# A two-block trunk on one core: lower weights subtracted on VectorE in the feed-forwards, and a bias table stored once and read shifted

## The chip, the cores and the metric

One Trainium2 core runs the whole program in one launch. The metric is the device time of that launch in microseconds: the median of three runs of the kernel before is 3242.26 (3242.16 to 3242.72). TensorE does the matrix products, VectorE (DVE) and ScalarE (ACT) the element-wise work, GpSimd (POOL) some of it, and SyncE (SP) issues most DMAs.

## The reference, cut to what matters

Two models run one after the other on 512 tokens of width 1024 in float32, each of two layers: a hybrid of two attentions with a convolutional feed-forward, then a state-space model beside windowed attention with another feed-forward.

```
def conv_ffn(h, w_up, conv_w, conv_b, w_down):          # first model
    u = h @ w_up                                         # 1024 -> 2 * 2816
    c = conv_b + sum over k < 3 of conv_w[k] * up[:, k:k + s]
    a, val = split(c, 2)
    return (gelu(a) * val) @ w_down                      # 2816 -> 1024

x = x + rms_norm(mixed @ w_out, attn_post_gain)          # a norm behind each half of a layer
h = rms_norm(x, ffn_pre_gain)
x = x + rms_norm(conv_ffn(h, ...), ffn_post_gain)

rel = arange(KEY_SPAN)[None, :] - WINDOW - arange(ATTN_BLOCK)[:, None]        # second model
band_bias = rel_bias[t5_bucket(rel)].transpose(2, 0, 1)   # (16 heads, 128 queries, 384 keys)
```

The bias depends on key minus query alone, so a head has one row of values, and the table's row for a query is that row shifted by the query's place.

## The kernel before, in words

**Exact products out of two halves.** Every weight block (128 x 128) and every activation is held as a rounded part and what is left of it: `wh` and `wl`, `h` and `hl` (`ah`, `al` for the products of a feed-forward). A product takes three matmuls (`mm3`, lines 489 to 491): `wh` with `h`, `wl` with `h`, `wh` with `hl`, all 512 columns wide.

**The stream of weights.** The host packs the weight blocks in the order of use into 460 chunks of eight blocks (512 KB), so TensorE spends 24 matmuls on a chunk. `Stream` brings them in. When the first block of chunk c is asked for, `load` issues the raw loads up to chunk c + 6 on SP (four buffers `wraw`), and `conv` turns chunk c + 3 into its halves (four buffers each of `wh` and `wl`): ScalarE writes the negated raw weights into `wl` (line 311), GpSimd issues a DMA that adds the weights from memory to it, and ScalarE rounds the raw weights into `wh` (line 316; GpSimd does that in the attention stages). Each engine works through its instructions in the order in which this code issues them (the schedule is manual), and so does each DMA queue: an instruction that waits holds up all behind it.

**The stages around the change.** A layer of the first model ends with the product with `w_out` (eight outputs), `post_norm`, a feed-forward, and `post_norm` again. `post_norm` sums squares (`sq`, `stat`), takes the root on ScalarE, spreads the factor over the partitions by four transposes (`statb`), and then for each of eight tiles scales `y`, adds it to `x` (VectorE for even tiles, GpSimd for odd ones), and splits `x` into `h` (ScalarE) and `hl` (VectorE). `keep_warm` gives TensorE small matmuls (`warm`) meanwhile. Behind it, `dense_group` works on four accumulators at once, block row by block row, over four chunks, so that it can begin with the first `h`; the squares for the next norm (`sq`) are taken between its block rows.

A feed-forward is 22 pairs of outputs (`pair`, two chunks each) with a product down (`down`, eleven chunks) behind pair 12 and one behind the last. An output of the first model is scaled (`u`, line 1225, VectorE), multiplied and biased (`c`, ScalarE), and gets two convolution steps (lines 1230 and 1232, VectorE); a pair then gets its gelu (ScalarE), product, rounded half `ah` (ScalarE) and lower half `al` (VectorE), deferred to the following blocks of weights. The second model's pair has one convolved output (lines 1851 to 1860) and one that is only scaled (`up`).

**The bias table.** `bias_table` is a generator that others step with `side.step`. It makes the 16 rows by one matmul (`btab`), stores them, loads each head back shifted by one element per partition (`brev`), turns the order of the partitions round by a matmul with an exchange matrix (`bex`), copies that on ScalarE (`bout`), and stores it to `bias_d`. Its steps stand in the first layer's `w_out` product and, four each, in the four calls of `post_norm`. The attention of the second model loads `bias_d` head by head.

Of the kernel before, what the change touches and what calls it, by code (L numbers as in the profile page):

```python
# [17 lines left out]
T = 512  # L18
# [6 lines left out]
NB, NO = 2, 2  # L25
XD = 30
GA, GB, GC = 1, 4, 1
NWU, NKW = 13, 6
NEG = -1.0e30
BIG = 3.0e38  # L30
TINY = 1e-30
# [102 lines left out]
assert NTILES % CH == 0  # L134
NCHUNK = NTILES // CH


def _pack_weights(arrs):
    out = np.zeros((NCHUNK, 128, CH, 128), np.float32)
# [13 lines left out]
def _consts():  # L153
    parts = []
    pos = 0

    def add(name, a):
        nonlocal pos
        a = np.asarray(a, np.float32)
        _CS[name] = (pos, a.shape[1])  # L160
        parts.append(a)
        pos += a.shape[1]

    p = np.arange(128)
    r, c = p[:, None], p[None, :]
    add("ident", np.eye(128))
    add("exch", np.eye(128)[::-1])
    add("maskA", np.concatenate([np.where(c > r, 0, NEG), np.where(c <= r, 0, NEG)], 1))
    add("maskC", np.concatenate([np.zeros((128, 384)), np.where(c <= r, 0, NEG)], 1))
    add("le", r <= c)  # L170
    add("ge", r >= c)
    add("gt", r > c)
    add("lt", r < c)
    n = np.arange(32)
    ok = np.stack([((n * 16 + 31)[None, :] <= (128 * i + p)[:, None]) & (n < 31)[None, :] for i in range(4)], 1)
    add("c01", ok.reshape(128, 128))
    add("cneg", np.where(ok, 0, NEG).reshape(128, 128))
    add("invf", (10000.0 ** (-(p % 32) / 32.0))[:, None])
    add("sign", np.where(p % 64 < 32, -1.0, 1.0)[:, None])
    return np.concatenate(parts, 1)  # L180
# [66 lines left out]
def trunk_kernel(ctx: ExitStack, tc: tile.TileContext, xT, positions, wts, cst_d, oh_d, rb_d, cw1_d,  # L247
# [14 lines left out]
    def big(name, dt=F32):  # L262
        return pools["t"].tile([128, T], dt, tag="t", name=name)
# [7 lines left out]
    def bank(name, hold=False):  # L271
        b = banks.pop(0)
        t = psum.tile([128, T], F32, tag=f"b{b}", name=name)
        if hold:
            held[id(t)] = (b, t)
        else:
            banks.append(b)
        return t
# [7 lines left out]
    class Stream:  # L286
        LOAD, CONV = 7, 3

        def __init__(self):
            self.t = 0  # L290
            self.loaded = 0
            self.conved = 0
            self.raw = {}
            self.hl = {}
            self.later = []

        def load(self, upto):
            while self.loaded < min(upto, NCHUNK):
# [3 lines left out]
                self.raw[c] = r  # L302
                self.loaded += 1

        def conv(self, upto):
            while self.conved < min(upto, NCHUNK):
                c = self.conved
                r = self.raw.pop(c)
                h = wpool.tile([128, CH * 128], F32R, tag="wh", name="wh", bufs=4)
                lo = wpool.tile([128, CH * 128], F32R, tag="wl", name="wl", bufs=4)  # L310
                A.activation(lo, r, AF.Copy, scale=-1.0)  # L311
                G.dma_start(out=lo, in_=wts[c], accum_op=OP.add)  # L312
                if busy["act"]:
                    G.tensor_copy(h, r)
                else:
                    A.activation(h, r, AF.Copy)  # L316
                self.hl[c] = (h, lo)
                self.conved += 1

        def defer(self, n, fn):  # L320

# [13 lines left out]
        def next(self, key):  # L335
            self.due(self.t)
            c, i = divmod(self.t, CH)
            if i == 0:
                self.load(c + self.LOAD)
                self.conv(c + self.CONV + 1)  # L340
                self.hl.pop(c - 1, None)
            name, l, r, cols = PLAN[self.t]
            assert (name, l, r) == key[:3], (PLAN[self.t], key)
            self.t += 1
            h, lo = self.hl[c]
            s = slice(128 * i, 128 * i + 128)
            return h[:, s], lo[:, s]
# [39 lines left out]
    def C(name):  # L387
        o, n = _CS[name]
        return cst[:, o:o + n]
# [394 lines left out]
    def layer1(l, x, hs, sq, gnext, side):  # L784
# [417 lines left out]

        x = load_x()
        for m in range(KT):
            if l == 0 and m in (1, 3, 4):
                side.step(1)
            g = dense(key("w_out", l), ms, out_evac)
            if m == KT - 1:
                run_some(g, 4)
                sq2.sums(1)  # L1210
                warm_sqrt()
            run(g)
# [23 lines left out]
            return f  # L1236

        def pair(i):
            if i == 0:
                dense_group(key("ffn_w_up", l), hs, [conv(0, "a0"), conv(FT, "v0"), conv(1, "a1"),  # L1240
                                                     conv(FT + 1, "v1")],
                            sq3, st3, x)
                x.clear()
            elif i > 1:
                run(dense(key("ffn_w_up", l), hs, conv(i, f"a{i}")))
                run(dense(key("ffn_w_up", l), hs, conv(FT + i, f"v{i}")))
            later(i, gated)
# [81 lines left out]

    def post_norm(x, ys, gcol, sq, gnext, side):  # L1330

        side.step(1)
        r4 = rstd_a(sq, D, act=True)
        side.step(1)
        R = spread(r4)
        side.step(2)
        keep_warm(NKW)
        hs, sqn, f = prep(x, gnext)
        for m in range(KT):
            y = ys[m]  # L1340
            V.scalar_tensor_tensor(y, y, gcol[:, m:m + 1], R, op0=OP.mult, op1=OP.mult)
            (V if m % 2 == 0 else G).tensor_add(x[m], x[m], y)
            if m:
                f(m - 1)
        f(KT - 1)
        free(R)
        return hs, sqn


    bias_d = dpool.tile([128, 16, 384], F32, name="bias_d")  # L1350

    def bias_table():

        oh = big("oh")
        nc.sync.dma_start(oh[0:33, :], oh_d)
        rb = small(16, "rb", bufs=2)
        nc.sync.dma_start(rb[0:32, :], rb_d)
        V.memset(rb[32:33, :], NEG)
        yield
        ps = bank("btab")  # L1360
        PE.matmul(ps[0:16, :], rb[0:33, :], oh[0:33, :], start=True, stop=True)
        tb_ = big("btab")
        V.tensor_copy(tb_[0:16, :], ps[0:16, :])
        tab_d = dpool.tile([16, T], F32, name="tab_d")
        nc.sync.dma_start(tab_d, tb_[0:16, :])
        rev = {}
        for h in range(18):
            if h < 16:
                rev[h] = big("brev")
                nc.sync.dma_start(rev[h][:, 0:384], bass.AP(  # L1370
                    tensor=tab_d.tensor, offset=tab_d.offset + h * T, ap=[[1, 128], [1, 384]]))
            if h >= 2:
                pb = bank("bex")
                PE.matmul(pb[:, 0:384], C("exch"), rev.pop(h - 2)[:, 0:384], start=True, stop=True)
                o = big("bout")
                A.activation(o[:, 0:384], pb[:, 0:384], AF.Copy)
                nc.sync.dma_start(bias_d[:, h - 2, :], o[:, 0:384])
            yield

    masks = []  # L1380
# [7 lines left out]
    def layer2(l, x, hs, sq, gnext):  # L1388
# [398 lines left out]
        def load_bias(h):  # L1787
            if h < 16:
                bias[h] = big("bias")
                nc.sync.dma_start(bias[h][:, 0:384], bias_d[:, h, :])  # L1790

        bias["load"] = load_bias
        load_bias(0)
# [218 lines left out]
```

## Time and profile before

| | |
|---|---|
| median of three runs | 3242.26 us |
| the profiled execution | 3243.99 us, its span 3242.2 us |
| mean granted TensorE clock | 0.980 |
| chunks of weights | 460, each loaded raw (512 KB) and added once more (512 KB) |
| DMA traffic | 547.30 MB, of it 241.20 MB in the queue of the adding DMAs |

A busy TensorE is not TensorE at its peak; a DMA share is the mean of 16 engines, rough where it goes over 1. Idle time of an engine that nobody waits for costs nothing. A wait for several semaphores is put down to the one that came last.

### The profile page before, as it was taken

To read this page: it belongs to the slowest core of one execution; us is meant where nothing else is said; L and a number is where in the kernel's file an instruction comes from. 1 tells how busy PE (TensorE), PEld (TensorE's weight loads), DVE (VectorE), ACT (ScalarE), POOL (GpSimd) and SP (SyncE) were. 2 spreads that over 40 slices of the span, in tenths; PEclk is the share of its full clock that TensorE was granted. 3 is DMA by queue.
4 is the path that set the end of the run, shared out by engine and by line. 5 is a ranking of instruction groups with operands and counts; after the bars stand their busy time and mean duration, and the time that the engine had idled before them with its cause. 6 is when DMAs were issued, how large, how long until landed. Compare 5 with 4: busy or idle time off the path is not lost. (4 is left out here: it accounts for less than half of the span.)

```text
span 3242.2 us, 40684 instructions
## 1 busy us (share of the span) xinstructions
PE 3104.8 (96%) x14604; PEld 2542.0 (78%) x14604; DVE 1681.9 (52%) x3431; ACT 1885.8 (58%) x3288; POOL 758.1 (23%) x770
## 2 busy tenths in 40 slices
PE   8999999999999999999999889999999988999998
PEld 7878878887778877888786668788888666878887
DVE  5577355153577735424376786331326678734132
ACT  4568556464457756645467577554556766755453
POOL 2222211111222211111125432111112552211110
PEclk9999999999999999999999999999999999999999
DMA  9744769887864487989775435789897534478975
GB/s 272 173 105 92 189 175 207 194 192 198 228 161 110 86 216 182 203 190 221 181 177 117 107 87 115 197 193 220 194 227 167 127 89 105 108 195 206 221 185 139
DMA packets 170277, 547.30 MB, mean 169 GB/s; under 512 B 20011, under 2 KB 29227, under 8 KB 170076
## 3 DMA queue, kind: packets, MB, share of 16 engines
q0 software_dynamic: 66240, 241.20, 43.9%
q1 hardware_dynamic: 103836, 303.50, 27.0%
q8 instruction: 116, 1.90, 0.2%
q14 instruction: 85, 0.70, 0.1%
HBM read 516.81 MB, written 19.96 MB: 166 GB/s over the span
## 5 line engine op out<-in xcount | busy, mean ns | idle before, releaser
L490 PE MATMUL acc<-h,wl 128*128 128x512 f32 x2464 | 975.2, 396 | 34.1 <-DMA wl<-in_wts 34.0
L489 PE MATMUL acc<-h,wh 128*128 128x512 f32 x2464 | 997.8, 405 | 3.5 <-DVE dm L1670 2.1
L491 PE MATMUL acc<-hl,wh 128*128 128x512 f32 x2464 | 973.3, 395 | 0.1
L312 POOL DMA_DIRECT2D wl<-in_wts x460 | 398.6, 867 | 2037.6 <-ACT wl L311 1845.3
L311 ACT ACTIVATE wl<-wraw 128x1024 fp32r<-128x1024 f32 x460 | 482.8, 1050 | 283.3 <-PE acc L490 257.6
L490 PEld LDWEIGHTS acc<-h,wl 128*128 128x128 f32 x2464 | 471.1, 191 | 133.4 <-DMA wl<-in_wts 40.8
L491 PEld LDWEIGHTS acc<-hl,wh 128*128 128x128 f32 x2464 | 469.8, 191 | 101.7 <-DVE hl L404 1.0
L489 PEld LDWEIGHTS acc<-h,wh 128*128 128x128 f32 x2464 | 471.5, 191 | 99.5 <-issue 5.3
L316 ACT ACTIVATE wh<-wraw 128x1024 fp32r<-128x1024 f32 x400 | 417.4, 1043 | 0.0
L489 PE MATMUL acc<-ah,wh 128*128 128x512 f32 x704 | 274.2, 390 | 0.0
L491 PE MATMUL acc<-al,wh 128*128 128x512 f32 x704 | 273.9, 389 | 0.0
L490 PE MATMUL acc<-ah,wl 128*128 128x512 f32 x704 | 273.9, 389 | 0.0
L674 PE MATMUL pt<-cst,p 128*128 128x128 f32 x752 | 143.6, 278 | 25.6 <-ACT p L1939 10.8
L1229 ACT ACTIVATE c<-u,prm 128x512 f32<-128x512 f32 x88 | 71.2, 815 | 144.3 <-DVE u L1225 144.3
L491 PEld LDWEIGHTS acc<-al,wh 128*128 128x128 f32 x704 | 132.1, 188 | 27.5
L489 PEld LDWEIGHTS acc<-ah,wh 128*128 128x128 f32 x704 | 132.1, 188 | 27.4
L490 PEld LDWEIGHTS acc<-ah,wl 128*128 128x128 f32 x704 | 132.1, 188 | 27.4
L1225 DVE TENSOR_TENSOR u<-acc,R 128x512 f32<-128x512 f32 x88 | 59.9, 687 | 172.5 <-PE acc L491 172.5
L1085 ACT ACTIVATE p<-p,nm 128x128 f32<-128x128 f32 x192 | 102.1, 532 | 62.6 <-DVE nm L1083 60.7
L680 ACT ACTIVATE pth<-pt 128x256 fp32r<-128x256 f32 (+2 forms) x320 | 130.8, 411 | 9.3 <-PE pt L674 6.8
L674 PEld LDWEIGHTS pt<-cst,p 128*128 128x128 f32 x752 | 93.0, 141 | 52.8 <-ACT p L1939 19.0
L1417 DVE SCALAR_TENSOR_TENSOR c<-u,prm,c 128x510 f32<-128x510 f32 (+2 forms) x120 | 98.5, 821 | 41.0 <-POOL c L1411 37.6
(334 smaller groups left out, 4944.9 us busy)
## 6 DMA issues: line engine op xcount, KB each, us to landing
wraw<-in_wts SPq DMA_DIRECT2D x460, 512.0 KB, 6.7
wl<-in_wts POOLq DMA_DIRECT2D x460, 512.0 KB, 7.2
bias<-bias_d SPq DMA_DIRECT2D x32, 192.0 KB, 2.5
x<-in_xT SPq DMA_DIRECT2D x16, 256.0 KB, 8.2
cw<-in_cw SPq DMA_DIRECT2D x16, 256.0 KB, 4.7
xf<-x SPq DMA_DIRECT2D x16, 256.0 KB, 2.2
x<-xf SPq DMA_DIRECT2D x16, 256.0 KB, 10.6
xs<-x SPq DMA_DIRECT2D x16, 256.0 KB, 5.7
```

The lines of the kernel that those rows point to most:

```text
L311: A.activation(lo, r, AF.Copy, scale=-1.0)
L312: G.dma_start(out=lo, in_=wts[c], accum_op=OP.add)
L316: A.activation(h, r, AF.Copy)
L489: PE.matmul(acc, wh, xh, start=first, stop=False)
L490: PE.matmul(acc, wl, xh, start=False, stop=False)
L491: PE.matmul(acc, wh, xl, start=False, stop=last)
L674: PE.transpose(pt[:, 128 * n:128 * n + 128], t[:, 128 * (kb - b0):128 * (kb - b0) + 128], ident)
L680: A.activation(th[:, 0:w], pt[:, 0:w], AF.Copy)
L1085: A.activation(p[:, 0:w], p[:, 0:w], AF.Exp, bias=nm[:, col:col + 1], scale=-1.0, accum_out=den[:, col:col + 1])
L1225: V.tensor_mul(u, acc, st3["R"])
L1229: A.activation(c, u, AF.Identity, bias=cb[:, idx:idx + 1], scale=cw[:, 88 + idx:89 + idx])
L1417: V.scalar_tensor_tensor(c[:, lo:hi], u[:, lo + d:hi + d], cw[:, 12 * k + idx:12 * k + idx + 1], c[:, lo:hi], op0=OP.mult, op1=OP.add)
```

## The change

In `conv`, chunks that `BYV` marks get their `wl` as raw minus `wh` by a VectorE instruction in place of the negation and the adding DMA, and their `wh` always from ScalarE. Marked are the first eight chunks and every chunk that belongs to a feed-forward together with the three before it: 260 of 460. A subtraction is issued one chunk later than the rounding that it needs (`subs`), except at the start and where unmarked chunks follow. The bias table is no longer turned round: each of the 16 rows is stored 128 times over, once for each partition, out of the one partition that holds it, and the attention reads it with a step of one element less than a row per partition. The steps stand in the pairs of the first layer's feed-forward; `post_norm` holds three and nine `warm` matmuls instead of the table's steps and six.

```diff
-NWU, NKW = 13, 6
+NWU, NKW = 13, 9
+_UP = ("ffn_w_up", "w_up_2", "ffn_w_down", "w_down_2")
+_FF = [all(t[0] in _UP for t in PLAN[CH * c:CH * c + CH]) for c in range(NCHUNK)]
+BYV = [c < 8 or all(_FF[max(0, c - 3):c + 1]) for c in range(NCHUNK)]
...
-        def conv(self, upto):
+        def conv(self, upto, later=False):
             while self.conved < min(upto, NCHUNK):
...
-                A.activation(lo, r, AF.Copy, scale=-1.0)
-                G.dma_start(out=lo, in_=wts[c], accum_op=OP.add)
-                if busy["act"]:
+                if BYV[c]:
+                    self.subs.append((lo, r, h))
+                else:
+                    A.activation(lo, r, AF.Copy, scale=-1.0)
+                    G.dma_start(out=lo, in_=wts[c], accum_op=OP.add)
+                if busy["act"] and not BYV[c]:
                     G.tensor_copy(h, r)
                 else:
                     A.activation(h, r, AF.Copy)
...
+            while len(self.subs) > (1 if later and BYV[self.conved - 1] else 0):
+                lo, r, h = self.subs.pop(0)
+                V.tensor_sub(lo, r, h.bitcast(F32))
...
-                self.conv(c + self.CONV + 1)
+                self.conv(c + self.CONV + 1, self.conved < NCHUNK - 1)
...
-            if l == 0 and m in (1, 3, 4):
-                side.step(1)
...
         def pair(i):
+            if l == 0 and i > 2:
+                side.step(1)
...
     def post_norm(x, ys, gcol, sq, gnext, side):
 
-        side.step(1)
         r4 = rstd_a(sq, D, act=True)
-        side.step(1)
+        keep_warm(3)
         R = spread(r4)
-        side.step(2)
         keep_warm(NKW)
...
-    bias_d = dpool.tile([128, 16, 384], F32, name="bias_d")
+    bias_d = dpool.tile([16, 128, T], F32, name="bias_d")
...
-        tab_d = dpool.tile([16, T], F32, name="tab_d")
-        nc.sync.dma_start(tab_d, tb_[0:16, :])
-        rev = {}
-        for h in range(18):
-            if h < 16:
-                rev[h] = big("brev")
-                nc.sync.dma_start(rev[h][:, 0:384], bass.AP(
-                    tensor=tab_d.tensor, offset=tab_d.offset + h * T, ap=[[1, 128], [1, 384]]))
-            if h >= 2:
-                pb = bank("bex")
-                PE.matmul(pb[:, 0:384], C("exch"), rev.pop(h - 2)[:, 0:384], start=True, stop=True)
-                o = big("bout")
-                A.activation(o[:, 0:384], pb[:, 0:384], AF.Copy)
-                nc.sync.dma_start(bias_d[:, h - 2, :], o[:, 0:384])
+        for h in range(16):
+            nc.sync.dma_start(bias_d[h], tb_[h:h + 1, None, :].to_broadcast([1, 128, T]))
             yield
...
-                nc.sync.dma_start(bias[h][:, 0:384], bias_d[:, h, :])
+                nc.sync.dma_start(bias[h][:, 0:384], bass.AP(
+                    tensor=bias_d.tensor, offset=bias_d.offset + h * 128 * T + 127, ap=[[T - 1, 128], [1, 384]]))
```

What this does to the order of instructions is shown at three places. The first is TensorE in the first `post_norm`, from the last blocks of `w_out` to the first of the feed-forward; before:

```order
L491 MATMUL acc<-ml,wh 128x512
L1374 MATMUL bex<-brev,cst 128x384
L434 MATMUL stat<-ones,sq 128x1 x4
L1374 MATMUL bex<-brev,cst 128x384
L473 MATMUL statb<-cst,rs 128x128 x4
L1374 MATMUL bex<-brev,cst 128x384 x2
L467 MATMUL warm<-ones 128x128 x6
L489 MATMUL acc<-h,wh 128x512
```

The same place on TensorE after the change:

```order
L501 MATMUL acc<-ml,wh 128x512
L444 MATMUL stat<-ones,sq 128x1 x4
L477 MATMUL warm<-ones 128x128 x3
L483 MATMUL statb<-cst,rs 128x128 x4
L477 MATMUL warm<-ones 128x128 x9
L499 MATMUL acc<-h,wh 128x512
```

The four matmuls of the table are gone, and six more small ones stand there. The second place is VectorE behind the eight tiles of that norm, in the first group of the feed-forward; before:

```order
L404 SCALAR_TENSOR_TENSOR hl<-x,prm,h 128x512 x2
L422 TENSOR_TENSOR sq<-sq 128x512 x6
L425 TENSOR_TENSOR sq<-sq 128x512
L443 TENSOR_REDUCE var<-stat 128x4
L451 TENSOR_SCALAR var<-var 128x4
```

The same place on VectorE after the change, where `wl<-wraw,wh` is the subtraction:

```order
L414 SCALAR_TENSOR_TENSOR hl<-x,prm,h 128x512 x2
L432 TENSOR_TENSOR sq<-sq 128x512 x2
L328 TENSOR_TENSOR wl<-wraw,wh 128x1024
L432 TENSOR_TENSOR sq<-sq 128x512 x4
L435 TENSOR_TENSOR sq<-sq 128x512
L328 TENSOR_TENSOR wl<-wraw,wh 128x1024 x2
L453 TENSOR_REDUCE var<-stat 128x4
```

The first subtraction stands between the adds of squares, two more ahead of the reduction of the next norm. The third place is VectorE in the middle of a feed-forward of the first model, one pair from an output's scaling to the next; before:

```order
L1225 TENSOR_TENSOR u<-acc,R 128x512
L1230 SCALAR_TENSOR_TENSOR c<-u,prm,c 128x511
L1232 SCALAR_TENSOR_TENSOR c<-u,prm,c 128x510
L1225 TENSOR_TENSOR u<-acc,R 128x512
L1230 SCALAR_TENSOR_TENSOR c<-u,prm,c 128x511
L1232 SCALAR_TENSOR_TENSOR c<-u,prm,c 128x510
L1294 TENSOR_TENSOR c<-c 128x512
L1299 TENSOR_TENSOR al<-c,ah 128x512
```

The same pair on VectorE after the change:

```order
L1233 TENSOR_TENSOR u<-acc,R 128x512
L1238 SCALAR_TENSOR_TENSOR c<-u,prm,c 128x511
L1240 SCALAR_TENSOR_TENSOR c<-u,prm,c 128x510
L328 TENSOR_TENSOR wl<-wraw,wh 128x1024
L1233 TENSOR_TENSOR u<-acc,R 128x512
L1238 SCALAR_TENSOR_TENSOR c<-u,prm,c 128x511
L1240 SCALAR_TENSOR_TENSOR c<-u,prm,c 128x510
L328 TENSOR_TENSOR wl<-wraw,wh 128x1024
L1304 TENSOR_TENSOR c<-c 128x512
L1309 TENSOR_TENSOR al<-c,ah 128x512
```

A subtraction has come in behind the convolution steps of each of the two outputs.

## Rows read from the trace of the kernel before

**Rows 1.** The page, busy time of each engine, its share, its instructions.

```profile
PE 3104.8 (96%) x14604; PEld 2542.0 (78%) x14604; DVE 1681.9 (52%) x3431; ACT 1885.8 (58%) x3288; POOL 758.1 (23%) x770
```

**Rows 2.** Waits of TensorE: line, releaser, us in total, times, longest.

```profile
PE acc L490 <- DMA wl<-in_wts: 34.0, 12, 6.7
...
PE btab L1361 <- DMA rb<-in_rel_bias: 0.8, 1, 0.8
```

**Rows 3.** Timeline, the start: start, duration (us), engine, line, operation, idle before.

```profile
5.41 1.04 ACT L316 ACTIVATE wh<-wraw 128x1024 fp32r<-128x1024 f32 x1
...
6.36 0.70 ACT L403 ACTIVATE h<-x,prm 128x512 fp32r<-128x512 f32 x1
...
14.28 0.80 PE L490 MATMUL acc<-h,wl 128*128 128x512 f32 x1 [6.66 <-DMA wl<-in_wts]
```

**Rows 4.** Windows: stretch, length, busy time and instructions by engine, clock, DMA share, GB/s.

```profile
14.00:19.00 5.00, 4.72 (x14) 3.82 (x15) 1.51 (x2) 3.14 (x4) 0.86 (x1) 0.63 1.06 316
...
443.00:448.00 5.00, 4.91 (x12) 3.90 (x13) 0.83 (x2) 2.95 (x4) 1.73 (x2) 0.52 1.05 261
...
2097.00:2103.00 6.00, 5.97 (x14) 4.72 (x15) 3.28 (x5) 4.34 (x7) 0.91 (x2) 0.50 0.74 163
```

**Rows 5.** Timeline, the first norm of the first layer, three engines.

```profile
416.80 0.69 DVE L1342 TENSOR_TENSOR x<-x,y 128x512 f32<-128x512 f32 x1
...
418.09 0.91 PE L1374 MATMUL bex<-brev,cst 128*128 128x384 f32 x2 [1.46 <-DMA brev<-tab_d]
...
419.42 1.32 ACT L403 ACTIVATE h<-x,prm 128x512 fp32r<-128x512 f32 x2
```

**Rows 6.** Timeline, the group of four accumulators behind it.

```profile
436.03 2.17 ACT L417 ACTIVATE sq<-x 128x512 f32<-128x512 f32 x4
...
437.71 1.29 DVE L422 TENSOR_TENSOR sq<-sq 128x512 f32<-128x512 f32 x2 [2.70 <-ACT sq L417]
...
443.09 0.79 PE L490 MATMUL acc<-h,wl 128*128 128x512 f32 x1 [5.73 <-DMA wl<-in_wts]
```

**Rows 7.** Timeline, the fourth norm, behind the second layer.

```profile
1585.26 0.69 DVE L1342 TENSOR_TENSOR x<-x,y 128x512 f32<-128x512 f32 x1
...
1588.93 1.32 ACT L403 ACTIVATE h<-x,prm 128x512 fp32r<-128x512 f32 x2
```

**Rows 8.** Timeline, the first groups of the second model's feed-forwards.

```profile
2087.73 0.69 DVE L1868 TENSOR_TENSOR up<-acc,R 128x512 f32<-128x512 f32 x1
...
2097.03 0.79 PE L490 MATMUL acc<-h,wl 128*128 128x512 f32 x1 [2.58 <-DMA wl<-in_wts]
...
2911.26 0.50 PE L490 MATMUL acc<-h,wl 128*128 128x512 f32 x1 [2.31 <-DMA wl<-in_wts]
```

**Rows 9.** Timeline of VectorE, one pair of the first feed-forward.

```profile
551.81 0.69 DVE L1225 TENSOR_TENSOR u<-acc,R 128x512 f32<-128x512 f32 x1 [1.78 <-PE acc L491]
...
555.80 0.69 DVE L1294 TENSOR_TENSOR c<-c 128x512 f32<-128x512 f32 x1 [0.88 <-ACT c L1251]
...
562.69 0.69 DVE L1225 TENSOR_TENSOR u<-acc,R 128x512 f32<-128x512 f32 x1 [1.78 <-PE acc L491]
```

**Rows 10.** Timeline, the first pairs of the first feed-forward.

```profile
464.52 0.69 DVE L1225 TENSOR_TENSOR u<-acc,R 128x512 f32<-128x512 f32 x1
...
491.73 0.50 PE L490 MATMUL acc<-h,wl 128*128 128x512 f32 x1 [0.54 <-DMA wl<-in_wts]
```

**Rows 11.** Timeline of VectorE, four adds of squares one behind another.

```profile
440.64 2.50 DVE L422 TENSOR_TENSOR sq<-sq 128x512 f32<-128x512 f32 x4 [1.64 <-ACT sq L417]
```

**Rows 12.** The page: SP's queue (packets, MB, share); an issue, KB, us to landing.

```profile
q1 hardware_dynamic: 103836, 303.50, 27.0%
...
xf<-x SPq DMA_DIRECT2D x16, 256.0 KB, 2.2
```

More of the change, by code (lines that the diff above doesn't have):

```diff
@@ L166, in _consts @@
     add("ident", np.eye(128))
-    add("exch", np.eye(128)[::-1])
     add("maskA", np.concatenate([np.where(c > r, 0, NEG), np.where(c <= r, 0, NEG)], 1))
@@ L295, in __init__ @@
             self.later = []
+            self.subs = []
         def load(self, upto):
```

## The prediction

> **What bounds the kernel.** I read the shares of the page first: TensorE is busy for 3104.8 of 3242.2 us [rows 1], so at most 137 us of waiting and some slow clock are to be had, and an engine that gets less work gives nothing by itself. The waits of TensorE come next: the longest group, 34.0 us in 12 pieces, is a matmul that waits for the DMA which makes the lower weights, `wl` [rows 2]. The timeline then shows where. One piece stands at the start: TensorE continues at 14.28 after 6.66 us of idleness [rows 3]. The large others stand about 17 us after a norm, in the first group of four accumulators: 5.73 us at 443.09 [rows 6], and 2.58 and 2.31 us at the second block's feed-forwards [rows 8]. [...]
>
> Elsewhere in the feed-forwards a chunk of 24 matmuls takes its 5.44 us without a gap, and VectorE waits for TensorE 1.78 us in each pair [rows 9]: nothing is won there, and something can be lost.
>
> **The change, part by part.**
>
> *The first eight chunks.* Before, ScalarE writes the negated weights, GpSimd issues an adding DMA, and only when this lands has TensorE its second matmul, at 14.28. Now ScalarE writes `wh` at 4.45 instead of 5.41 (the place of the removed negation), VectorE subtracts, 1.15 us (512-wide adds follow each other every 0.60 [rows 11]; 1024 columns are two of these less one start), so `wl` is there by 6.7; the matmul before it waits for `h`, at the latest 7.1, from 6.36 and 0.70 [rows 3]. The second matmul moves from 14.28 to about 7.3: 7.0, and 1.8 of low clock. What is late next is x and the raw chunks: the queues are full there (a DMA share of 1.06 at 316 GB/s [rows 4]), but three adding DMAs of 0.5 MB, some 5 us at that rate, go away ahead of the last pieces of x. VectorE gets two subtractions inside its chain after the norm; I charge one, 1.2. Term: 7.6.
>
> *The bias table in the norms.* Each of four norms held four `bex` matmul pairs and copies on ScalarE between the norm's own steps. In the first, x is ready at 417.49, but `h` starts at 419.42, behind a copy whose matmul had waited 1.46 us for a DMA [rows 5]: 1.93 us. In the fourth it is 1588.93 against 1585.95: 2.98 [rows 7]. The two others lie between; mean 2.45. The new `warm` matmuls stand where TensorE waits for the norm anyway. Behind the second and fourth norm no chunk is a feed-forward chunk, so the wait for `wl` stays, and only this moves: 2 x 2.45 = 4.9.
>
> *First group of the first block's feed-forwards (two).* VectorE's first subtraction stands after two of the six adds of squares. With the norm's shift of 1.93, ScalarE's squares begin at 436.03 - 1.93 - 0.95 (the second 0.95 is the negation dropped ahead of them) = 433.15; the two adds follow 1.68 later as before (437.71 less 436.03) and take 1.29; the subtraction ends at about 437.35. TensorE then goes on there instead of at 443.09: 5.7. [...] So 7.0, twice: 14.0.
>
> *First group of the second block's feed-forwards (two).* The subtraction that replaces the late DMA stands after the third pair of convolution steps and one product, so after 2087.73 + 0.6 and two subtractions, at 2090.6 [rows 8], and TensorE is there at 2094.3: the waits of 2.58 and 2.31 go, with about 4 us of low clock, less 0.3 for the subtraction of the chunk before, which now ends just as it is wanted. Term: 8.6.
>
> *The rest of the feed-forwards.* 252 subtractions come to VectorE. In a pair of the first block, its most loaded one, VectorE needs 10.88 - 1.78 = 9.1 us today, of which 0.88 is the wait for the activation [rows 9]. One subtraction is added whole (1.15), one falls in that wait (0.27): 10.5 of 10.88. It fits with 0.4 to spare; were the price two separate 512-wide instructions (1.38, two of 0.69 [rows 9], the upper end) it would be 11.0, and cost 0.1 a pair. I take 1.15. But the backlog after the norm now shrinks slowly. VectorE takes the first own pair at 464.52 [rows 10], 7 us behind TensorE (counted from 443.09 by chunks), and a subtraction must end within two chunks, 10.9 us, of the chunk it stands behind; with its convolution that takes 4.2, leaving 6.7. The first three pairs, which also hold the table load and three products, miss this by 0.2 to 1.1 each: 2 us per feed-forward, in place of waits for DMA of 0.5 [rows 10] and less. Net cost: 2 for both.
>
> *The table's stores.* The matmul that makes the table moves into a pair at its old cost; its wait for a small load goes [rows 2]: 0.8. Then 16 stores of 256 KB each read one partition 128 times, one in each of nine pairs and then of seven, on the queue that brings the raw weights. No row shows such a source. From below: 256 KB out of 128 partitions land in 2.2 us [rows 12], and the store is hidden. From above: if one partition gives no more than one of the 16 engines moves (303.5 MB in 27.0% of 3242 us by 16 engines: 21.7 GB/s), 12.1 us. A raw chunk takes 1.5 us of all engines by the same row, so a pair needs store + 3.0 against 10.88: free below 7.9 us, then the excess adds up, nine times and seven times, less the slack of four buffers and VectorE's 6.7 us (8 us in the first run, where the backlog has used a part, and 12 in the second). At 12.1 this is 4.2 x 9 - 8 + 4.2 x 7 - 12 = 47. I take 9.5, nearer to the upper end, since the rows at the lower one all spread over many partitions: 1.6 x 9 - 8 = 7, and nothing in the second run.
> [...]
>
> *Sum.* 7.6 + 4.9 + 14.0 + 8.6 - 2 + 0.8 - 7 = 26.9. The profiled execution took 3243.99 (span 3242.2), 1.7 above the median of 3242.26; taken off the execution this gives 3217, for the median 3215.
>
> **Rivals.**
> 1. *The stores are hidden* (they land in under 7.9 us): for it, the rows of 2.2 us; against it, that one partition feeds them. 3242.3 - 33.9 = 3208.
> 2. *The stores starve the first feed-forward* at 12.1 us each: raw chunks come late, `wh` waits, TensorE waits. It decides from about 11 us a store; against it, that it needs the slowest row price. 3208 + 47 = 3255, slower.
> 3. *VectorE becomes the bound of the first block's feed-forwards*: with 1.6 us per subtraction a pair needs 11.35, 0.47 too much, in 2 x 18 pairs: 17. For it, the margin of 0.4; against it, that the price of the same work is shown [rows 11]. 3232.
> 4. *The waits are handed on*: the start is then bound by x (its gain falls to 3), the groups by squares and the clock stays low after them (each gain halves): 3215 + 4.6 + 7 = about 3227. For it, full queues at the start.
>
> **How the numbers follow.** Forecast 0.40, rival 1 0.28, rival 2 0.10, rival 3 0.08, rival 4 0.14. The likeliest is 3215. The range reaches down past rival 1 by a few us for terms that are a little small, to 3202, and up past rival 3 into half of rival 2, to 3245. A change under 0.2% (6.5 us) is no change here. Faster: the forecast, rivals 1 and 4 and nearly all of 3, less some of each: 0.84; same 0.07; slower 0.09, nearly all rival 2.
>
> **What would show it.** In the changed profile: no wait for `wl` of 6 us at the start, TensorE's second matmul at about 7.3; the wait behind the first norm down to some 2 us, and none at the second block's; `h` right behind x in all four norms; a VectorE subtraction of about 1.15 us; VectorE without the 1.78 us wait in the first block's pairs. The landing time of the `bias_d` stores decides between forecast and rivals 1 and 2; a first feed-forward longer than that of the second layer by over 10 us would speak for rival 2. I am wrong if TensorE waits for `wl` from VectorE all through a feed-forward, or if the start still stalls on x.

## The result and the profile after the change

The changed kernel takes 3210.29 us (median; 3207.63 to 3211.24), the kernel before 3242.21 beside it: a ratio of 0.9900, 95% interval 0.9883 to 0.9917, thus 32 us faster. The profiled execution is the shortest of its runs, 3207.63 us with a span of 3205.9, and 36.3 us shorter in span than the one of before.

The page of the changed kernel, busy time by engine; it answers to [rows 1]:

```profile
PE 3084.3 (96%) x14620; PEld 2532.3 (79%) x14620; DVE 1974.5 (62%) x3691; ACT 1643.5 (51%) x3012; POOL 533.6 (17%) x510
```

VectorE got 293 us of work and lies far from full by this average. The waits of TensorE, against [rows 2]:

```profile
PE acc L500 <- DMA wl<-in_wts: 12.3, 2, 6.3
...
PE acc L500 <- DVE wl L328: 6.4, 7, 1.9
```

Ten of the twelve waits for the adding DMAs are gone; 34.0 us became 12.3 for two of these and 6.4 in seven waits for VectorE. The start, against [rows 3], as VectorE, then TensorE show it:

```profile
5.52 1.23 DVE L328 TENSOR_TENSOR wl<-wraw,wh 128x1024 fp32r<-128x1024 f32 x1 [4.51 <-ACT wh L323]
```

```profile
6.70 0.50 PE L499 MATMUL acc<-h,wh 128*128 128x512 f32 x1
7.03 0.40 PE L500 MATMUL acc<-h,wl 128*128 128x512 f32 x1
```

The second matmul comes at 7.03 instead of 14.28 (forecast: 7.3). The group behind the first norm, on TensorE, and behind the second norm:

```profile
423.91 0.50 PE L500 MATMUL acc<-h,wl 128*128 128x512 f32 x1 [1.88 <-DVE wl L328]
...
466.03 0.50 PE L500 MATMUL acc<-h,wl 128*128 128x512 f32 x1 [0.74 <-DVE wl L328]
...
802.89 0.80 PE L500 MATMUL acc<-h,wl 128*128 128x512 f32 x1 [5.99 <-DMA wl<-in_wts]
```

Behind the first norm the wait fell from 5.73 [rows 6] to 1.88. Behind the second one no chunk is marked, and the wait has grown: before, it was

```profile
823.90 0.79 PE L490 MATMUL acc<-h,wl 128*128 128x512 f32 x1 [4.88 <-DMA wl<-in_wts]
```

and behind the fourth norm it went from 4.72 to 6.27. The windows of the first 5 us of products and right behind the waits of 1.88 and 5.99 us, columns as in [rows 4]:

```profile
6.70:11.70 5.00, 4.95 (x21) 3.78 (x22) 3.39 (x6) 3.37 (x5) 0.00 (x0) 1.00 1.02 397
424.00:429.00 5.00, 5.00 (x22) 4.13 (x23) 4.96 (x7) 2.84 (x4) 0.00 (x0) 1.00 0.34 105
803.00:808.00 5.00, 5.00 (x12) 3.94 (x13) 0.39 (x1) 0.58 (x1) 0.79 (x1) 0.50 1.08 283
```

At the start no slow clock is left. After 1.88 us of waiting the granted clock is 1.00, and 22 matmuls fit into 5 us; after 5.99 us it is 0.50, and 12 fit. In the second model's first groups [rows 8] no wait is left. VectorE in the first pairs of the first feed-forward, which answers to [rows 9]:

```profile
509.12 0.68 DVE L1233 TENSOR_TENSOR u<-acc,R 128x512 f32<-128x512 f32 x1
510.69 0.75 DVE L1238 SCALAR_TENSOR_TENSOR c<-u,prm,c 128x511 f32<-128x511 f32 x1 [0.89 <-ACT c L1237]
511.48 0.75 DVE L1240 SCALAR_TENSOR_TENSOR c<-u,prm,c 128x510 f32<-128x510 f32 x1
512.14 1.22 DVE L328 TENSOR_TENSOR wl<-wraw,wh 128x1024 fp32r<-128x1024 f32 x1
...
518.82 0.69 DVE L1309 TENSOR_TENSOR al<-c,ah 128x512 fp32r<-128x512 f32 x1 [0.70 <-ACT ah L1307]
519.43 0.68 DVE L1233 TENSOR_TENSOR u<-acc,R 128x512 f32<-128x512 f32 x1
```

From `u` to `u` one pair takes 10.31 us with no wait for TensorE: VectorE is behind and catches up, 0.57 us of 10.88 per pair. A subtraction takes 1.22 us. The stores of the table and, for comparison, the table of DMA issues of [rows 12] after the change:

```profile
xf<-x SPq DMA_DIRECT2D x16, 256.0 KB, 2.0
bias_d<-btab SPq DMA_DIRECT2D x16, 256.0 KB, 11.3
```

A store out of one partition lands in 11.3 us, one out of 128 in 2.0; yet the first feed-forward is no longer than the second layer's (370.0 against 369.4 us).

Where the 36.3 us of span come from, read at the same matmuls (the `stat` and `statb` groups) in both timelines of TensorE:

| place | forecast | measured |
|---|---|---|
| start | 7.6 | 8.6 |
| norms 2 and 4 with their groups | 4.9 | 1.75 + 0.95 |
| first groups, first model's feed-forwards | 14.0 | 6.86 + 7.38 |
| first groups, second model's feed-forwards | 8.6 | 5.5 + 3.9 |
| rest of the feed-forwards, with the table's matmul | -1.2 | -1.67 - 1.03 |
| the table's stores | -7 | about 0 (experiments 3 to 5) |
| first attention of the first layer, of the second | 0, 0 | +5.9, -4.3 |
| all else | 0 | +2.4 |

Each row compares one execution of either kernel. Another execution of the changed kernel (experiment 11) has 1.83 + 2.86 in the second row and +0.1 in place of -4.3; in the other places named it agrees within 0.7.

### The profile page after: what moved, and what is told of

It is laid out like the page before. It is cut to its first block, busy times and chain, and to the rows that moved or that the text cites. A ratio compares the mean times of both kernels' runs of the same rounds, so it can differ in the third digit from the quotient of the medians.

```text
span 3205.9 us, 39992 instructions
## 1 busy us (share of the span) xinstructions
PE 3084.3 (96%) x14620; PEld 2532.3 (79%) x14620; DVE 1974.5 (62%) x3691; ACT 1643.5 (51%) x3012; POOL 533.6 (17%) x510
## 3 DMA queue, kind: packets, MB, share of 16 engines
q8 instruction: 115, 1.88, 0.2%
## 5 line engine op out<-in xcount | busy, mean ns | idle before, releaser
L500 PE MATMUL acc<-h,wl 128*128 128x512 f32 x2464 | 969.6, 394 | 18.7 <-DMA wl<-in_wts 12.3
L500 PEld LDWEIGHTS acc<-h,wl 128*128 128x128 f32 x2464 | 468.3, 190 | 115.9 <-DMA wl<-in_wts 13.1
L319 POOL DMA_DIRECT2D wl<-in_wts x200 | 174.3, 871 | 1888.5 <-ACT wl L318 1340.3
L328 DVE TENSOR_TENSOR wl<-wraw,wh 128x1024 fp32r<-128x1024 f32 x260 | 316.5, 1220 | 102.4 <-ACT wh L323 94.8
L318 ACT ACTIVATE wl<-wraw 128x1024 fp32r<-128x1024 f32 x200 | 210.0, 1050 | 80.7 <-PE acc L500 63.2
L500 PEld LDWEIGHTS acc<-ah,wl 128*128 128x128 f32 x704 | 132.2, 188 | 27.5
L1307 ACT ACTIVATE ah<-c 128x512 fp32r<-128x512 f32 x88 | 55.7, 633 | 137.8 <-DVE c L1304 137.6
## 6 DMA issues: line engine op xcount, KB each, us to landing
bias_d<-btab SPq DMA_DIRECT2D x16, 256.0 KB, 11.3
```

The lines of the kernel that those rows point to most:

```text
L328: V.tensor_sub(lo, r, h.bitcast(F32))
L500: PE.matmul(acc, wl, xh, start=False, stop=False)
L1307: A.activation(h, a, AF.Copy)
```

## Experiments: one part at a time

**1. The first eight chunks alone**: the kernel before with the change's code for the subtraction, and with this choice of chunks in it.

```diff
+BYV = [c < 8 for c in range(NCHUNK)]
```

> The kernel before with one part of the change: VectorE subtracts for chunks 0 to 7 alone. Theory A (the parts are independent, and the wait for the second compression weights in the first layer goes because the first eight chunks' adding DMAs go): 8.6 us at the start and 5.4 in the first layer's attention (a wait of 3.48 and 1.93 of low clock), together 14.0, so 3228. Rival B (that wait went with the other parts): 8.6 alone, 3234. Rival C (rival 4 of the prediction, the start is handed on to x): under 4, 3238 or more.

3229.53 us, ratio 0.9966 (0.9954 to 0.9977), 11 less than the kernel before beside it (3240.61). A expects a gain of 14.0 and B one of 8.6, so the time lies between them; C is out. The trace decides for the mechanism of A: the start gains 8.43, and another wait goes, that for the compression weights (`cw`, for the products `hid` in the first model's attention). The second group of these hidden products of the first layer, in the kernel before and in this one:

```profile
75.08 6.46 PE L870 MATMUL hid<-gt,cw 128*128 128x62 f32 x32 [3.48 <-DMA cw<-in_cw]
```

```profile
66.48 3.68 PE L881 MATMUL hid<-gt,cw 128*128 128x62 f32 x32
```

The wait for the second compression weights is gone here, and stays in the next two kernels (3.44 and 4.30), which leave the first eight chunks as they were. Of the 5.9 us that the forecast did not have (first attention of the first layer, in the table), 4.6 come with this part alone. In the second layer's first attention this execution loses 3.4 again, at a wait of the first hidden products for which the profile names no releaser:

```profile
840.92 6.57 PE L881 MATMUL hid<-gt,cw 128*128 128x62 f32 x32 [3.19 <-issue]
```

**2. The feed-forwards alone**, put on the kernel before in the same way.

```diff
+BYV = [c > 7 and all(_FF[max(0, c - 3):c + 1]) for c in range(NCHUNK)]
```

> The kernel before with one part of the change: VectorE subtracts for the chunks of the feed-forwards alone. Theory A: the first groups give 6.9 + 7.4 less the norms' shift of about 1.9 each, so 10.4, the second model's groups 9.4, the rest of the first model's feed-forwards costs 2.7: 17.1, so 3225, and the second layer's first attention loses nothing, because TensorE comes to it no earlier behind its norm. Rival B: the 4.3 us lost in that attention belong to the subtraction for the feed-forward ahead of it: 12.8, so 3229.

3225.76 us, ratio 0.9953 (0.9938 to 0.9967), 14.9 less than the kernel before beside it: between A (17.1) and B (12.8). The trace has a piece of each: the first model's groups give 4.51 and 6.28, together what A says (10.4), but 3.5 are lost in the second layer's first attention, where the compression weights come late:

```profile
864.55 7.06 PE L881 MATMUL hid<-gt,cw 128*128 128x62 f32 x32 [3.05 <-DMA cw<-in_cw]
```

So this loss needs neither the first chunks nor the norm's shift; and experiment 1 has one of that size in the same attention without the feed-forwards' subtractions.

**3. The bias table alone**: the changed kernel with all lower weights by adding DMAs.

```diff
-BYV = [c < 8 or all(_FF[max(0, c - 3):c + 1]) for c in range(NCHUNK)]
+BYV = [False for c in range(NCHUNK)]
```

> The kernel before with one part of the change: the bias table by shifted reads, its stores in the first feed-forward; all lower weights by adding DMAs, as before. In this feed-forward the DMA share is then 0.92 from the loads before a store is added. Theory A (a store occupies the 16 engines for about 6 us, 0.57 of a pair, and all that moves in a pair must fit into 10.88 us): 1.49 pairs of work per pair, 5.3 us over in each of 16 pairs, less some 8 of slack in each of two runs: the first feed-forward is about 65 us longer, the norms give 8 back, 3300. Rival B (a store goes beside the other loads and costs nothing, as it does after the change): the norms' gain alone, 8, so 3234. Rival C (the price of the prediction, 9.5 us in the queue that brings the raw weights, 1.6 over in a pair): some 7 to 30 us longer, 3240 to 3265.

3284.85 us, ratio 1.0135 (1.0116 to 1.0155): 44 **slower** than the kernel before. Its waits of TensorE:

```profile
PE acc L500 <- DMA wl<-in_wts: 69.0, 19, 7.4
```

The stretch from the first norm to the second is 432.3 us against 381.5 before. B (stores cost nothing) is wrong by 50 us; A gave 65 for that stretch, C at most 30. So the stores cost much where the adding DMAs run, and nothing where they do not (experiment 5): alone the parts make -11, -15 and +44, together they make -32.

**4. Two stores in a pair**, on the changed kernel.

```diff
             if l == 0 and i > 2:
-                side.step(1)
+                side.step(2)
```

> The changed kernel with two stores of the bias table in a pair in place of one, so that they end after eight pairs instead of sixteen. Theory A (a store occupies the engines for 6 us): 0.32 + 2 x 0.57 = 1.46, 5.0 us over in each of eight pairs, less some 8 to 12 of slack: 28 to 32 us longer, 3240. Rival B (stores go beside the loads and cost nothing): 3210, as after the change. Rival C (each holds the queue for its landing of 11.3 us): 2 x 11.3 + 3 against 10.88, 14.7 over in eight pairs, over 100 us longer.

3259.52 us, ratio to before 1.0059 (1.0042 to 1.0076), some 50 longer than the change. The stretch between the norms is 432.7 against 381.5; 10.15 of it is a wait for the table's own small load, now issued right ahead of its use. All three expectations miss: A by 20, B by 50, C by 50 and more. What a store costs is read from SP (start and duration of the issues). Between two pairs of stores stand two raw loads, and these wait for a buffer to come free (49.0 us of SP's waits end with VectorE's subtraction), so SP can't run far ahead of what has landed:

```profile
466.85 1.14 SPq L1373 DMA_DIRECT2D bias_d<-btab  x2
472.60 11.94 SPq L305 DMA_DIRECT2D wraw<-in_wts  x2
484.59 1.13 SPq L1373 DMA_DIRECT2D bias_d<-btab  x2
485.83 14.28 SPq L305 DMA_DIRECT2D wraw<-in_wts  x2
...
556.85 1.17 SPq L1373 DMA_DIRECT2D bias_d<-btab  x2
558.12 16.79 SPq L305 DMA_DIRECT2D wraw<-in_wts  x2
574.96 1.13 SPq L1373 DMA_DIRECT2D bias_d<-btab  x2
```

From 466.85 to 574.96 are six rounds, 18.02 us each, for two stores and two raw loads: 9.0 us a store, or 29 GB/s. The traffic of this kernel from 465 to 560 us, 40 slices of 2.4 us:

```profile
DMA  6999899888998878998899988988977999989888
GB/s 226 242 32 28 27 28 28 27 44 269 216 28 39 84 50 129 254 82 27 27 28 28 28 27 250 250 28 31 71 47 71 295 122 28 28 27 28 27 37 172
```

No slice is under 27 GB/s, so a store is under way nearly all the time. In the slices where only stores move it is 27 to 28 GB/s, though the engines show as eight or nine tenths busy: 256 KB at 27.5 are 9.5 us. Over a round with raw loads in it the stores get 29, no less. The raw loads thus go beside the stores and add nothing to the round; the DMA share, from which A took its 6 us, tells neither the price nor the room that is left.

**5. One store in place of sixteen**, on the changed kernel. The loads of all heads read the first head's row; the other fifteen rows are left out.

```diff
-            nc.sync.dma_start(bias_d[h], ...)
+            if h == 0:
+                nc.sync.dma_start(bias_d[0], tb_[0:1, None, :].to_broadcast([1, 128, T]))
...
```

> The changed kernel with one of the sixteen stores of the bias table alone; all heads read the first head's row, so the values of the other fifteen are left out. Theory A (a store occupies the engines for about 6 us, which fits beside a feed-forward's other loads once the adding DMAs are gone): the stores cost nothing there, and the first feed-forward stays as it is, 370 us: 3210, at most 1 less. Rival C (the price of the prediction, 7 us): 3203.

3209.00 us, ratio to before 0.9904 (0.9889 to 0.9919): the same as with all sixteen (0.9900, and 0.9903 in experiment 11). From the group behind the first norm to that behind the second it is 0.7 longer, not shorter. On the changed kernel the stores are free.

**6. Every subtraction twice**, on the changed kernel.

```diff
                 V.tensor_sub(lo, r, h.bitcast(F32))
+                V.tensor_sub(lo, r, h.bitcast(F32))
```

> The changed kernel with every subtraction on VectorE made twice in a row, 1.22 us each. It asks for VectorE's margin in the first model's feed-forwards. Theory A (the sum of the prediction with the measured price: 9.1 + 1.22 + 1.22 - 0.88 = 10.66 us of 10.88 per pair): 13.1 per pair, 2.2 over in some 20 pairs of each of two feed-forwards, less about 6 of lag that is allowed in each of four stretches between them: 64 us longer, 3274, with VectorE's subtraction as what TensorE waits for. Rival B (VectorE has room that the sum doesn't see, 1.5 us a pair or more): less than 20 longer, under 3230.

3311.49 us, ratio to before 1.0222 (1.0206 to 1.0237), 101 longer than the change. The waits of TensorE, and two starts of a pair on VectorE:

```profile
PE acc L501 <- DVE wl L329: 69.6, 43, 3.2
```

```profile
507.80 0.68 DVE L1234 TENSOR_TENSOR u<-acc,R 128x512 f32<-128x512 f32 x1
...
520.63 0.68 DVE L1234 TENSOR_TENSOR u<-acc,R 128x512 f32<-128x512 f32 x1
```

A pair takes 12.83 us, VectorE is the bound, and TensorE waits in nearly every one. Theory A has the mechanism and is short by 37 us: it takes off a lag of 6 us in each of four stretches, 24 in all, of which the trace shows little, and it leaves out the second model. The first model's stretches between norms are 41.3 and 39.3 longer, 1.95 for each of some 20 pairs and little off; about 11 lie in the second model's.

## Experiments: what the change left

**7. Compression weights earlier.**

```diff
+            if j == 1:
+                load_cw1(1)
             if j == 2:
                 gk = add_pos(0, cw[0])
             if j == 3:
                 hidden(0, gk)
-                load_cw1(1)
```

> The changed kernel with the loads of the second compression weights issued two outputs earlier, ahead of eight of the swap loads on the same queue. Theory A (in the second layer's first attention the loads are late because they are issued 15 us behind TensorE's first hidden product, at 844.12, when TensorE wants them at 844.4): the wait of 3.93 goes, and with it 2.5 of slow hidden products and some clock: 5 to 7 us less, 3204. Rival B (the wait is handed to the swap loads that are now later, or to the instruction that follows): within 2 us of 3210.

3203.20 us, ratio to before 0.9888 (0.9871 to 0.9904); the kernel of experiment 5 on the same chip had 0.9904. In the second layer the hidden products, first of the change, then of this version:

```profile
848.32 6.29 PE L880 MATMUL hid<-gt,cw 128*128 128x62 f32 x32 [3.93 <-DMA cw<-in_cw]
```

```profile
844.10 3.68 PE L880 MATMUL hid<-gt,cw 128*128 128x62 f32 x32
```

The wait is gone and that attention is 5.0 shorter than in the execution shown above (0.6 shorter than in that of experiment 11, where the wait was 0.63); a wait for lower weights of 2.96 has come at 868.24, and of the 4.8 that this execution is ahead behind that layer's attention 1.2 are left at the end. The intervals of the times overlap: alone it is inconclusive.

**8. The subtraction ahead of the squares, and for chunks 118 and 233 too.**

```diff
+BYV = [c < 8 or c in (118, 233) or all(...) for c in range(NCHUNK)]
+NOW = (52, 118, 167, 233)
...
-            while len(self.subs) > (1 if later and BYV[self.conved - 1] else 0):
+            while len(self.subs) > (1 if later and BYV[self.conved - 1]
+                                    and self.conved - 1 not in NOW else 0):
```

> The changed kernel where VectorE also subtracts for the fourth chunk of the group behind the second and the fourth norm (chunks 118 and 233), and where in the first group behind all four norms the subtraction stands ahead of the adds of squares. Theory A (these groups wait for the lower weights alone, 5.99, 6.27 and twice 1.88 us, with low clock behind the two long ones): 1.88 twice and 6 twice go, and about 2 of clock twice, together 18 to 20: 3191, unless the waits for the compression weights grow by the same as TensorE comes earlier. Rival B (something else is late there, squares or the chunk behind it): half of that or less, 3200 or more.

3200.11 us, ratio to before 0.9878 (0.9863 to 0.9893): half of what A expects, thus B. The first model's feed-forward groups gain 2.2 each, as A says. From the groups behind norms 1 and 3 to those behind norms 2 and 4 the gain is 7.4 and 8.3, of which 4.1 and 4.5 are lost right behind the group:

```profile
804.92 0.79 PE L501 MATMUL acc<-h,wl 128*128 128x512 f32 x1 [2.46 <-DMA wl<-in_wts]
...
1583.01 0.80 PE L501 MATMUL acc<-h,wl 128*128 128x512 f32 x1 [2.79 <-DMA wl<-in_wts]
```

The next chunk still comes by an adding DMA, and is late now.

**9. VectorE subtracts for chunks 118 to 121 and 233 to 236**, on the kernel of experiment 8.

```diff
-BYV = [c < 8 or c in (118, 233) or all(...) for c in range(NCHUNK)]
+BYV = [c < 8 or c in (118, 119, 120, 121, 233, 234, 235, 236) or all(...) for c in range(NCHUNK)]
```

> The version with the subtraction ahead of the adds of squares, with VectorE subtracting for chunks 118 to 121 and 233 to 236 in place of 118 and 233 alone. Theory A (there the wait was handed to the next chunk, which still came by an adding DMA: 2.46 us at 804.92 and 2.79 at 1583.01, with the low clock behind them 4.1 and 4.5): these go too, 8.6 beyond that version's 10: about 3191. Rival B (the time is handed on once more, to the compression weights or to a chunk behind 121): 3197 or more.

3189.81 us, ratio to before 0.9844 (0.9829 to 0.9858): theory A. What norms 2 and 4 gain (7.8 and 9.4) stays behind the group. Its waits of TensorE:

```profile
PE hid L881 <- DMA cw<-in_cw: 4.1, 1, 4.1
...
PE acc L501 <- DVE wl L329: 3.1, 7, 0.7
```

No wait for lower weights by DMA is left; the one for the compression weights still stands.

**10. The same with the compression weights earlier.**

> The same with the loads of the second compression weights issued two outputs earlier. Theory A (the two gains add up): 4 to 6 less than the version without, about 3186. Rival B (the earlier loads delay raw chunks or adding DMAs, as a wait of 2.96 for lower weights at 868.24 in the version with them alone suggests): within 2 of the version without.

3184.90 us, ratio to before 0.9828 (0.9813 to 0.9842). By its median 4.9 less, as A says; the intervals overlap, so the times alone do not settle it. In the trace the wait of 4.1 is gone, and TensorE has no wait for the lower weights over 0.7.

**11. Seven chunks instead of four**, on the kernel of experiment 10.

> The same with VectorE subtracting for chunks 118 to 124 and 233 to 239. Theory A (what TensorE waits for behind the group is the adding DMA): 1 to 3 less than with four chunks. Rival B (VectorE waits there for DMAs itself, 3.7 and 2.8 us before it adds the positions, and a subtraction behind them is late): 2 or more longer than with four chunks, with TensorE waiting for VectorE's subtraction.

3184.32 us, ratio to before 0.9825 (0.9810 to 0.9840): neither theory; the three chunks more make no difference. These two are the fastest versions, 55 us under the kernel before and 24 under the change, which was run beside them:

> The changed kernel itself, on the same chip as the three versions of it, so that they can be compared with it: 3210 by every theory.

3208.71 us (3202.54 to 3210.67), ratio to before 0.9903 (0.9887 to 0.9920). Its second layer's hidden products:

```profile
847.58 3.75 PE L880 MATMUL hid<-gt,cw 128*128 128x62 f32 x32 [0.63 <-DMA cw<-in_cw]
```

In this execution the wait was 0.63, not 3.93. With the loads in their old place it is over 3 us in six of the profiled kernels with VectorE subtracting in the feed-forwards (the change, experiments 2, 4, 5, 6 and 9), short in two (this one and experiment 8), and absent in the three without (before, experiments 1 and 3). In experiments 1 and 8 it is the first hidden products of that layer that wait, 3.19 and 2.90 us, without a releaser. So the loss of 4.3 in the table belongs to some executions, not to all.

## Why the prediction held, and which step of it failed

The forecast was 3215, the time is 3210.3, and it lies 2 from rival 1 (3208), whose end came true without its condition (a landing under 7.9 us; it is 11.3). That the total comes so near is in part luck: 7 us charged for the stores and 5.9 gained in an attention without a forecast stand against 4.3 lost in another, 2.2 missing behind the norms and 1.5 in the feed-forwards.

- **Start: right.** `wl` at 6.7 and the matmul at 7.03, no low clock (1.00 in the first 5 us from 6.70). 8.6 for 7.6: without the 1.2 that I charged for VectorE's chain the term had been 8.8.
- **What it missed at the start's edge.** I let the removed adding DMAs speed up x, and looked no further along the queues. In the first layer the weights issued at 70.8 made TensorE wait 3.48; that this wait goes with the first eight chunks is shown (experiment 1). How, whether by the emptier queues or because SP issues earlier, was not tried apart: the loads stood 33.3 us behind the norm's `stat` before and 27.3 after.
- **Norms: the shift was read at the wrong element.** `h` does stand right behind x now (403.05 for 403.01 in norm 1). But I took the shift of the *first* `h`, 1.93 to 2.98. From VectorE's first product with `R` to the first `h`, norm 1 gained 1.89, as forecast. To the *last* `h` it is 17.48 us before and 16.61 after: 0.87. The rows on ScalarE in the changed kernel show why:

```profile
410.13 1.34 ACT L413 ACTIVATE h<-x,prm 128x512 fp32r<-128x512 f32 x2 [2.41 <-POOL x L1350]
414.13 1.34 ACT L413 ACTIVATE h<-x,prm 128x512 fp32r<-128x512 f32 x2 [2.67 <-POOL x L1350]
418.15 0.72 ACT L413 ACTIVATE h<-x,prm 128x512 fp32r<-128x512 f32 x1 [2.68 <-POOL x L1350]
```

  Two tiles take 4.0 us, paced by the adds on GpSimd, in both kernels (429.48 to 433.50 before). The early tiles' gain melts against them. In norms 2 and 4 the last `h` gains 1.24 and 1.91, where 2.45 was charged. The negation on ScalarE stands behind the last `h`, and the adding DMA that TensorE waits for behind the negation (793.02, 793.64 and 794.99 in norm 2): so the waits grew there (5.99 for 4.88, 6.27 for 4.72). In norm 4 the new `warm` matmuls, charged with nothing, also hold up `statb`; the granted clock is 0.66 there (1558 to 1563), and VectorE's first product with `R` comes 3.69 us behind the second `stat`, 2.54 before:

```profile
1559.67 1.63 PE L477 MATMUL warm<-ones 128*128 128x128 f32 x6
1561.09 1.06 PE L483 MATMUL statb<-cst,rs 128*128 128x128 f32 x4
```

  So 2.7 came instead of 4.9 in this execution. How much the term is worth is not settled: another execution has 4.7 (experiment 11), and experiment 1, with the norms as before, has 1.08 + 1.89 in the same places.
- **First groups: right in sum**, 14.2 for 14.0 and 9.4 for 8.6, the first by two errors that cancel. Counted from the norm's `stat`, TensorE goes on 4.70 and 5.06 us earlier behind norms 1 and 3, where 5.7 was forecast; behind that point 2.16 and 2.32 more are gained, where the 7.0 holds 1.3 beside the 5.7; no slow clock is left (1.00, against 0.52 [rows 4]). The remaining wait, 1.88, is what I had called about 2.
- **Low clock: estimates of mine.** No run shows by themselves the 1.8 in the start's term, the 1.3 of the first groups or the about 4 in the 8.6 for the second model. They rest on [rows 4]: 14, 12 and 14 matmuls there fill 5.00, 5.00 and 6.00 us at 0.63, 0.52 and 0.50, where at 0.227 each (10.88 for 48 [rows 9]) they would take an estimated 1.8, 2.3 and 2.8 less. In their place the changed kernel shows 21 and 22 matmuls in 5.00 us at 1.00 (at the start and behind norm 1) and, where the second model's wait of 2.58 stood, 28 in 6.00:

```profile
2070.00:2076.00 6.00, 6.00 (x28) 4.99 (x27) 5.20 (x7) 3.16 (x4) 0.00 (x0) 1.00 0.24 87
```

- **VectorE: right.** 1.22 for 1.15 us, 10.31 for 10.5 a pair, a backlog that costs 2.7 where I had 1.2 net with the table's matmul; rival 3 is refuted for this price, and experiment 6 shows that it would have come true at a price twice as high. Its sum was a little low: 9.1 + 2 x 1.6 - 0.88 is 11.42, not 11.35.
- **Stores: the step that failed.** Not the price: 9.5 us was forecast, an estimate of mine between 2.2 and 12.1 that no run had shown, and 9.0 to 9.5 are measured (27 to 28 GB/s in experiment 4). It is the sentence "a pair needs store + 3.0 against 10.88: free below 7.9" that is wrong. Store and raw loads do not add up on this queue, they go beside each other (18.02 us a round; the sum says 2 x 9.5 + 3.0 = 22.0). By that a store is free below an estimated 10.9 us, the length of a pair, where no adding DMAs run. The term of -7 is 0. The landing time, 11.3, which I had named as the judge between the cases, judges nothing: it holds the time in which others moved too (from 465 to 560 us in experiment 4 the median is 16.9, at 9.0 a store).
- **Rival 2** (starvation) needs the adding DMAs still in place, or two stores in a pair; experiments 3 and 4 show both. **Rival 4** (the waits are handed on) did not come at the start or in the marked groups, which gained what was forecast; it came behind norms 2 and 4, where the waits grew, and in experiment 8.

Open: in experiment 3 the issues of the stores go 13.1 us apart on average (486.04 to 590.65, eight rounds), unevenly, from 6.2 to 26.0. Neither "beside" (no more than 10.88) nor the sum of the DMA shares (1.49 x 10.88 = 16.2) gives that. Why an adding DMA hinders a store and a raw load does not was not found; nor why the second layer's hidden products wait in some executions and not in others.

## What to carry to other kernels

Price a gain at the last element that the waiting engine needs, not at the first. Transfers with a narrow source and transfers with a wide one need not add up (two of each in 18.02 us here, for a sum of 22.0): before summing them, put two of the suspect ones into a period and read the period from the issuing engine, since here neither the landing time (11.3 us) nor the DMA share (0.8 to 0.9) gave the price, 9.0. And a change with several parts can hide that one of them is harmful alone: here the bias table cost 44 us alone and its stores nothing beside the other parts.

## What the runs showed of the hardware

- Stores of 256 KB out of one partition moved at 27 to 28 GB/s in slices of their own and showed the 16 DMA engines as 0.8 to 0.9 busy; 512 KB loads into 128 partitions passed beside them in slices of 250 to 295 GB/s, and over a round with two such loads the stores got 29 GB/s (experiment 4).
- One such store in each pair cost 51 us over a feed-forward's stretch beside adding DMAs (432.3 for 381.5, experiment 3), and nothing without them (one store in place of sixteen: 0.7 longer, experiment 5).
- Behind a wait of 1.88 us TensorE's granted clock was 1.00 over 5 us (424 to 429), behind one of 5.99 us it was 0.50 (803 to 808).
